# Starting two stationary operands at bytes 108 and 364 instead of 32 modulo 512

## The chip, the core and the metric

The kernel runs on one core of a Trainium2 chip. The metric is the device time of one execution in microseconds. In the profile PE is TensorE's matrix multiplication, PEld its loading of the stationary operand, DVE VectorE, ACT ScalarE, POOL GpSimd and SP SyncE. Each engine has its own stream of instructions and they wait for each other by semaphores; DMA queues move data between memory (HBM) and the on-chip memory (SBUF). SBUF has 128 partitions; a tile takes the same range of bytes in each of them, and "byte 32 modulo 512" below is where a tile's or a slice's range begins in every partition.

## What is computed

The reference is a two-layer decoder trunk on 256 tokens of width 2048, in float32. Each layer is a token mixer (layer 0 a gated DeltaNet, layer 1 HGRN2) followed by a SwiGLU block; each part is preceded by an RMSNorm and added to its input, and a last RMSNorm ends it:

```python
for layer in range(DEPTH):                       # DEPTH = 2
    h = h + mixer(rmsnorm(h, ...), ...)          # gated DeltaNet, then HGRN2
    h = h + swiglu(rmsnorm(h, ffn_norm[layer]), ffn_w_gate[layer], ffn_w_up[layer], ffn_w_down[layer])
return rmsnorm(h, final_norm)

def swiglu(h, w_gate, w_up, w_down):
    return (jax.nn.silu(h @ w_gate) * (h @ w_up)) @ w_down     # 2048 -> 5632 -> 2048
```

The change lies in the two SwiGLU blocks, in the product with `w_gate` and `w_up`.

## The kernel before

**High and low halves.** Every large product is computed from two halves of each operand: the high half is the float32 value rounded to the format that TensorE multiplies in one pass (`float32r`, a ScalarE copy), the low half what the rounding left out (a VectorE subtraction). A product takes three matmuls: high by high, high by low, low by high. Weights come by DMA in tiles of 128 x 1024 (`raw`, 512 KB) into four buffers, are split into `wh` and `wl` (four buffers each), and are used once. The tokens' halves stay on chip: `xt_h` and `xt_l`, four tiles each of 128 x (4 x 256), with the 2048 features along partitions and tiles and the 256 tokens along the free axis.

**Two ways of multiplying.** In `mm_rows` the tokens are stationary (128 x 128, loaded into TensorE) and 512 columns of weights stream past them. In `mm_cols` a 128 x 128 block of weights is stationary and the 256 tokens stream. `mm_cols` is used for part of the two mixers' input products (1024 triples of matmuls), `mm_rows` for nearly all else.

**Strassen's algorithm.** A SwiGLU block has 22 groups of 256 gate and 256 up columns, worked on in 11 pairs. Of each block, pairs 1, 4, 7 and 8 (`FF_PLAN`) are computed by a form of Strassen's algorithm with seven products in place of eight (`mixed_group`): the tokens are cut in two halves of 128, the features in two halves of 1024, the columns in gate and up. Three products (1, 2 and 4) take plain token halves from `xt_h` and `xt_l`. The other four (3, 5, 6 and 7) take sums of token blocks, which `mix_inputs` prepares once at the start of a block: VectorE forms the sums, ScalarE writes their high halves and VectorE their low halves into the tiles `mixh` and `mixl`, four sums of 1024 columns each. In every matmul of these groups the stationary operand is 128 columns of `mixh`, `mixl`, `xt_h` or `xt_l`, and the moving operand is 256 columns of `wh` or `wl`. The weights of products 4 to 7 are themselves sums, formed by VectorE in the weight tile before it is split. A group has four times four items; the `parts` of an item tell its products, so the items are: product 1; products 2 and 3 in turn; 5 and 7; 6 and 4 in turn. Each item has 6 or 12 matmuls, in triples that share a slice of tokens. `among` sets these items singly between the items (12 matmuls of 512 columns) of the plain pairs or of the down product.

**Order.** The program first records all operations. A planner (`plan`) then places them by modelled costs and due times into one order, which is issued engine by engine; weight tiles are prepared ahead of the matmuls, up to the number of buffers. The cost of an operation depends on its shape and not on where its tiles lie.

**Where tiles lie.** Pools are allocated in order, a tile after the other. A phase's pool (`ffn0`, `ffn1`) places its tiles in order of first use, with those whose size is no multiple of 512 bytes last (`open`). Constants are sized so that `xt_h` and `xt_l` begin at byte 32 modulo 512, and the phases' large tiles do too, `mixh` and `mixl` included (16,384 bytes each, first in their phase). The `wh` and `wl` buffers are longer by `PAD` = 64 words, and `make` shifts the slice that is used: for `mm_rows` and the mixed groups it begins at 32 modulo 512; for `mm_cols` at 108 (`wh`) and 364 (`wl`):

```python
PAD = 64
IN_COLS = {"wh": 108, "wl": 364}
...
at = 32 + n * v.pad * 4 % 512
want = IN_COLS[v.tag] if v.cols else 32 + n % 2 * 512
v.skip = (want - at) // 4
```

**Tail.** After the last down product `finish` and `finish_last` apply the last norm. They reuse the two tiles' places: `last` (the norm's weights, loaded by GpSimd's queue) in the place of `mixl`, and the output rows `y` in that of `mixh`.

The recorder calls one helper for all operations, so the profile has one line (L496) for nearly all instructions and the groups are told apart by the names of their tiles: `aux<-wh,mixh` is a matmul into `aux` with `wh` moving and `mixh` stationary.

Of the kernel before, what the change touches and what calls it, by code (L numbers as in the profile page):

```python
# [8 lines left out]
F32 = mybir.dt.float32  # L9
F32R = mybir.dt.float32r  # L10
# [7 lines left out]
P = 128  # L18
T = 256
D = 2048  # L20
# [61 lines left out]
PAD = 64  # L82
# [440 lines left out]
class Trunk:  # L523
# [308 lines left out]
    def mix_inputs(self):  # L832

        nc = self.nc

        def tt(out, a, b, op):
            nc.vector.tensor_tensor(out=out, in0=a, in1=b, op=op)

        self.mixed = [[], [], [], []]
        both = [self.tile(self.pool, [P, 4096], f"mix{x}", F32R) for x in "hl"]  # L840
        row = self.rstd_row.unsqueeze(1).broadcast_to([P, 4, T])
        for q in range(2):
            uv = []
            for cg in (q, 2 + q):
                t = self.tile(self.pool, [P, 4, T], "turned", bufs=2, ordered=True)
                tt(t, self.xt_h[cg].bitcast(F32), self.xt_l[cg].bitcast(F32), ALU.add)
                tt(t, t, row, ALU.mult)
                uv += [t[:, :, 0:P], t[:, :, P:T]]
            a11, a21, a12, a22 = uv
            sums = []  # L850
            for _ in range(2):
                t = self.tile(self.pool, [P, 2, 512], "h1", bufs=2, ordered=True)
                sums += [t[:, i, :].rearrange("p (k t) -> p k t", k=4) for i in range(2)]
            s1, s2, s3, s4 = sums
            tt(s1, a21, a22, ALU.subtract)
            tt(s2, a11, s1, ALU.subtract)
            tt(s3, a21, a11, ALU.subtract)
            tt(s4, a12, s2, ALU.subtract)
            for n in range(4):
                h, low = (  # L860
                    m[:, (2 * n + q) * 512 : (2 * n + q + 1) * 512].rearrange("p (k t) -> p k t", k=4)
                    for m in both
                )
                nc.scalar.activation(h, sums[n], AF.Copy)
                tt(low, sums[n], h.bitcast(F32), ALU.subtract)
                self.mixed[n].append((h, low))
# [994 lines left out]
    def finish(self, cg):  # L1861
        nc = self.nc
        if cg == 0:
            self.last = self.tile(self.pool, [P, 4096], "mixl", F32R, ordered=True).bitcast(F32)[:, 0:D]
            nc.gpsimd.dma_start(self.last, self.a["final_norm"].broadcast_to([P, D]))
            self.y = self.tile(self.pool, [P, 4096], "mixh", F32R, ordered=True).bitcast(F32).rearrange("p (t c) -> p t c", t=2)
            self.part = self.tile(self.pool, [P, 2], "part")
        self.sumsq(cg)
        c = slice(cg * 512, (cg + 1) * 512)
        nc.vector.tensor_tensor(  # L1870
            out=self.y[:, :, c], in0=self.x[cg], in1=self.last[:, c].unsqueeze(1).broadcast_to([P, 2, 512]),
            op=ALU.mult,
        )
        if cg == 2:
            nc.vector.tensor_reduce(
                out=self.part, in_=self.ssp[:, :, 0:3], axis=mybir.AxisListType.X, op=ALU.add
            )
            nc.vector.tensor_scalar(
                out=self.part, in0=self.part, scalar1=1.0 / D, scalar2=EPS, op0=ALU.mult, op1=ALU.add
            )  # L1880
# [130 lines left out]
```

## Time and profile before

| | |
|---|---|
| median of 3 runs | 2747.35 us (2745.71 to 2747.43) |
| the profiled execution | 2747.26 us |
| its span | 2745.6 us |
| TensorE busy, in matmuls | 2727.6 us, 16,822 instructions |
| weight loads | 2363.9 us, 16,822 instructions |
| VectorE busy | 2169.4 us |
| ScalarE busy | 1548.5 us |
| HBM traffic | 605.92 MB by DMA packets, mean 221 GB/s |
| mean granted TensorE clock | 0.998 |

The span runs from the first to the last instruction of the profiled execution; its own time is longer by what lies around the span. A row of a group reads: line, engine, operation, output<-inputs, array size, shape, count | busy us, mean ns of one | idle us of the engine just before, and what ended it. A matmul's duration reaches from its start to the end of its pipeline, so those of neighbours overlap, and the time that a matmul costs in a stream is the distance to the next one's start. A row of the view in order of time begins with the start in us and the duration in us.

### The profile page before, as it was taken

The page shows a single profiled execution, that of the slowest core. Times are in us where ns is not written, and L with a number is a line of the kernel's source. Part 1 is how long each engine was busy: PE and PEld are TensorE (multiplying, and loading weights), DVE is VectorE, ACT ScalarE, POOL GpSimd, SP SyncE. Part 2 cuts the span into 40 slices and gives each one's busy share as a digit, 9 for nine tenths or more (in the row PEclk, how much of TensorE's full clock was granted, in tenths as well). Part 3 has the DMA queues.
Part 4 walks back from the last instruction along what each step waited for, and adds up shares of the span by engine and source line. Part 5 has one row for each costly group of instructions (what it writes and reads, how often), then busy time and mean ns, then how long its engine had stood idle before and what let it go on. Part 6 is the DMA issues. An engine that isn't in the chain of part 4 may idle for free.

```text
span 2745.6 us, 44285 instructions
## 1 busy us (share of the span) xinstructions
PE 2727.6 (99%) x16822; PEld 2363.9 (86%) x16822; DVE 2169.4 (79%) x3309; ACT 1548.5 (56%) x2192; POOL 308.4 (11%) x466
## 2 busy tenths in 40 slices
PE   9999999999999999999999999999999999999998
PEld 9888888888888888888888989988888888888887
DVE  6778888877769898889857688778678898888665
ACT  6646666566555555555545556556455555555443
POOL 1213222232110000000000100000100000000000
PEclk9999999999999999999999999999999999999999
DMA  7686578686676667766676655555676667676764
GB/s 258 201 280 225 182 219 278 215 273 223 221 249 226 218 210 242 238 216 216 224 234 220 225 167 182 170 167 179 226 264 208 216 222 237 222 228 218 250 210 167
DMA packets 170375, 605.92 MB, mean 221 GB/s; under 512 B 21674, under 2 KB 22842, under 8 KB 170032
## 3 DMA queue, kind: packets, MB, share of 16 engines
q1 hardware_dynamic: 138912, 503.15, 55.9%
q0 software_dynamic: 30960, 99.08, 11.4%
q8 instruction: 132, 2.16, 0.3%
q10 hardware_dynamic: 288, 0.85, 0.1%
q14 instruction: 83, 0.68, 0.1%
HBM read 563.10 MB, written 39.89 MB: 220 GB/s over the span
## 4 chain that ended last, share of the span: by engine, by line
PE 98%; ACT 0%; DVE 0%; issue 0%; DMA 0%; SPq 0%; POOLq 0%; POOL 0%; ACTq 0%
PE main L496 81%; PE aux L496 18%; DMA first<-in_x 0%; ACT dec L496 0%; DVE wl L496 0%; ACT wh L496 0%; DVE utmp L496 0%; SPq L496 0%; DVE pre L496 0%; ACT xt_h L496 0%; DVE u L496 0%; ACT mixh L496 0%; POOLq L2007 0%; ACT junk L496 0%; DVE p L496 0%
## 5 line engine op out<-in xcount | busy, mean ns | idle before, releaser
L496 ACT ACTIVATE wh<-raw 128x1024 fp32r<-128x1024 f32 x817 | 864.4, 1059 | 937.9 <-PE main L496 803.2
L496 DVE TENSOR_TENSOR wl<-raw,wh 128x1024 fp32r<-128x1024 f32 x817 | 1003.1, 1229 | 426.4 <-ACT wh L496 416.8
L496 PE MATMUL main<-wh,xt_h 128*128 128x512 f32 x1664 | 651.8, 392 | 0.8 <-ACT wh L496 0.8
L496 PE MATMUL main<-wl,xt_h 128*128 128x512 f32 x1664 | 651.0, 391 | 1.3 <-DVE wl L496 1.3
L496 PE MATMUL main<-wh,xt_l 128*128 128x512 f32 x1664 | 650.6, 391 | 0.0
L496 PEld LDWEIGHTS main<-wh,xt_l 128*128 128x128 f32 x1664 | 312.6, 188 | 65.2
L496 PEld LDWEIGHTS main<-wh,xt_h 128*128 128x128 f32 x1664 | 312.9, 188 | 62.8 <-ACT wh L496 1.2
L496 PEld LDWEIGHTS main<-wl,xt_h 128*128 128x128 f32 x1664 | 312.9, 188 | 61.4 <-DVE wl L496 1.6
L496 ACT ACTIVATE wh<-sraw 128x1024 fp32r<-128x1024 f32 (+1 forms) x256 | 243.4, 951 | 141.6 <-PE main L496 98.1
L496 DVE TENSOR_TENSOR wl<-sraw,wh 128x1024 fp32r<-128x1024 f32 (+1 forms) x256 | 278.4, 1088 | 28.2 <-ACT wh L496 26.8
L496 PE MATMUL main<-xt_h,wh 128*128 128x256 f32 (+1 forms) x1040 | 289.5, 278 | 0.7 <-ACT wh L496 0.7
L496 PE MATMUL main<-xt_h,wl 128*128 128x256 f32 (+1 forms) x1040 | 288.9, 278 | 0.9 <-DVE wl L496 0.9
L496 PE MATMUL main<-xt_l,wh 128*128 128x256 f32 (+1 forms) x1040 | 288.7, 278 | 0.3 <-DVE xt_l L496 0.3
L496 PE MATMUL main<-wh,hth 128*128 128x512 f32 x680 | 266.7, 392 | 1.0 <-ACT hth L496 1.0
L496 PE MATMUL main<-wl,hth 128*128 128x512 f32 x680 | 266.2, 391 | 0.0
L496 PE MATMUL main<-wh,htl 128*128 128x512 f32 x680 | 265.5, 390 | 0.1
L496 PEld LDWEIGHTS main<-xt_h,wh 128*128 128x128 f32 (+1 forms) x1040 | 194.8, 187 | 1.3 <-ACT wh L496 0.9
L496 PEld LDWEIGHTS main<-xt_h,wl 128*128 128x128 f32 (+1 forms) x1040 | 194.7, 187 | 1.2 <-DVE wl L496 1.1
L496 PEld LDWEIGHTS main<-xt_l,wh 128*128 128x128 f32 (+1 forms) x1040 | 194.7, 187 | 1.0 <-DVE xt_l L496 0.5
L496 PEld LDWEIGHTS main<-wh,htl 128*128 128x128 f32 x680 | 127.7, 188 | 29.1 <-DVE htl L496 1.7
L496 PE MATMUL main<-wh,ot_l 128*128 128x512 f32 x384 | 151.4, 394 | 0.0
L496 PE MATMUL main<-wh,ot_h 128*128 128x512 f32 x384 | 150.6, 392 | 0.0
(238 smaller groups left out, 4094.0 us busy)
## 6 DMA issues: line engine op xcount, KB each, us to landing
raw<-in_ffn_gu SPq DMA_DIRECT2D x224, 512.0 KB, 4.6
raw<-in_ffn_d SPq DMA_DIRECT2D x176, 512.0 KB, 4.6
sraw<-in_ffn_gu SPq DMA_DIRECT2D x128, 512.0 KB, 5.1
raw<-in_hgrn_in SPq DMA_DIRECT2D x128, 512.0 KB, 3.9
raw<-in_gdn_kq SPq DMA_DIRECT2D x64, 512.0 KB, 5.7
raw<-in_gdn_v SPq DMA_DIRECT2D x64, 512.0 KB, 4.8
raw<-in_gdn_z SPq DMA_DIRECT2D x64, 512.0 KB, 4.8
raw<-in_gdn_out SPq DMA_DIRECT2D x64, 512.0 KB, 5.0
```

The lines of the kernel that those rows point to most:

```text
L496: getattr(getattr(tc.nc, op.eng), op.method)(*args, **kw)
```

## The change

The tiles `mixh` and `mixl` become 64 words longer, and the sums are written to and read from words 19 to 4114 of them. With the place that the allocator then gives the tiles (last in their phase, 16,640 bytes each), the high halves begin at byte 108 and the low halves at byte 364 modulo 512, and so does every 128-column slice, since the slices are multiples of 512 bytes apart. The other tiles of the phase move down by 32,768 bytes and keep their place modulo 512. `finish` takes the longer tiles and uses them from their first word: `last` lies at 288 and `y` at 32 modulo 512. No instruction is added or removed, and the planner's order is the same.

```diff
@@ mix_inputs
-        both = [self.tile(self.pool, [P, 4096], f"mix{x}", F32R) for x in "hl"]
+        both = [self.tile(self.pool, [P, 4096 + PAD], f"mix{x}", F32R)[:, 19 : 19 + 4096] for x in "hl"]
@@ finish
-            self.last = self.tile(self.pool, [P, 4096], "mixl", F32R, ordered=True).bitcast(F32)[:, 0:D]
+            self.last = self.tile(self.pool, [P, 4096 + PAD], "mixl", F32R, ordered=True).bitcast(F32)[:, 0:D]
             nc.gpsimd.dma_start(self.last, self.a["final_norm"].broadcast_to([P, D]))
-            self.y = self.tile(self.pool, [P, 4096], "mixh", F32R, ordered=True).bitcast(F32).rearrange("p (t c) -> p t c", t=2)
+            self.y = self.tile(self.pool, [P, 4096 + PAD], "mixh", F32R, ordered=True).bitcast(F32)[:, 0:4096].rearrange("p (t c) -> p t c", t=2)
```

## The prediction

> **What bounds the kernel now.** I read the page first (share of the span, then the chain), then the groups by form of TensorE, then the two FFN stretches by engine, and last single matmuls in order of time.
>
> ```profile
> span 2745.6 us, 44285 instructions
> PE 2727.6 (99%) x16822; PEld 2363.9 (86%) x16822; DVE 2169.4 (79%) x3309; ACT 1548.5 (56%) x2192; POOL 308.4 (11%) x466
> PE 98%; ACT 0%; DVE 0%; issue 0%; DMA 0%; SPq 0%; POOLq 0%; POOL 0%; ACTq 0%
> ```
>
> The chain that ends last is 98% TensorE. What shortens a matmul's turn on TensorE shortens the kernel, as long as the engines that feed it keep up. The operands of the change belong to the groups below (stationary operand last in the name), with their weight loads; beside them stand the only other groups whose moving operand also has 256 columns.
>
> ```profile
> L496 PE MATMUL main<-xt_h,wh 128*128 128x256 f32 x1024 | 284.3, 278 | 0.7 <-ACT wh L496 0.7
> L496 PE MATMUL aux<-wh,mixh 128*128 128x256 f32 x512 | 144.4, 282 | 0.0
> L496 PE MATMUL aux<-wl,mixh 128*128 128x256 f32 x512 | 144.9, 283 | 0.0
> L496 PE MATMUL aux<-wh,mixl 128*128 128x256 f32 x512 | 145.0, 283 | 0.0
> L496 PE MATMUL aux<-wh,xt_h 128*128 128x256 f32 x384 | 108.1, 282 | 0.0
> L496 PEld LDWEIGHTS main<-xt_h,wh 128*128 128x128 f32 x1024 | 192.3, 188 | 1.3 <-ACT wh L496 0.9
> L496 PEld LDWEIGHTS aux<-wh,mixh 128*128 128x128 f32 x512 | 97.9, 191 | 4.4
> L496 PEld LDWEIGHTS aux<-wh,xt_h 128*128 128x128 f32 x384 | 73.3, 191 | 4.4
> ```
>
> So 3 x 512 = 1536 matmuls have a sum of tokens as the stationary operand, and TensorE sat idle 0.0 us before them. By the program's layout, every operand of the `aux` rows starts at byte 32 modulo 512, stationary and moving alike. In the `main<-xt_h,wh` row the stationary operand is a weight tile at 108 (`wh`) or 364 (`wl`), and the moving one, the tokens, is at 32. There the load takes 188 ns against 191, the matmul 278 against 282. These durations overlap; the cost is the distance between starts. Matmuls in order of time, first a run of 12 on sums between 512-column matmuls, then one that alternates sums and plain tokens:
>
> ```profile
> 1005.64 0.39 PE L496 MATMUL main<-wh,htl 128*128 128x512 f32 x1
> 1005.87 0.28 PE L496 MATMUL aux<-wh,mixh 128*128 128x256 f32 x1
> 1005.98 0.28 PE L496 MATMUL aux<-wl,mixh 128*128 128x256 f32 x1
> 1006.10 0.28 PE L496 MATMUL aux<-wh,mixl 128*128 128x256 f32 x1
> ...
> 1007.18 0.28 PE L496 MATMUL aux<-wh,mixl 128*128 128x256 f32 x1
> 1007.30 0.40 PE L496 MATMUL main<-wh,hth 128*128 128x512 f32 x1
> ...
> 1010.28 0.28 PE L496 MATMUL aux<-wh,mixl 128*128 128x256 f32 x1
> 1010.40 0.28 PE L496 MATMUL aux<-wh,xt_h 128*128 128x256 f32 x1
> ...
> 1011.36 0.28 PE L496 MATMUL aux<-wh,xt_l 128*128 128x256 f32 x1
> 1011.48 0.40 PE L496 MATMUL main<-wh,hth 128*128 128x512 f32 x1
> ```
>
> From 1006.10 to 1007.30 are 10 matmuls in 1.20 us: 120 ns each; from 1010.40 to 1011.48 are nine, half sums and half plain tokens, in 1.08 us: 120 ns again. The start of a run is cheaper: 1005.87 to 1006.10 is 0.23 us for two matmuls instead of 0.24, so a run of 12 takes 1.43 us. Between the roundings I take 7 ns. Now the run with weights stationary at 108 and 364, which also enters from 512 columns:
>
> ```profile
> 471.38 0.39 PE L496 MATMUL main<-wh,ot_l 128*128 128x512 f32 x1
> 471.61 0.28 PE L496 MATMUL main<-xt_h,wh 128*128 128x256 f32 x1
> ...
> 471.96 0.28 PE L496 MATMUL main<-xt_h,wh 128*128 128x256 f32 x1
> ...
> 482.73 0.28 PE L496 MATMUL main<-xt_h,wl 128*128 128x256 f32 x1
> ```
>
> The first three take 0.35 us, 117 ns each. From the fourth to the last of these 99 are 95 distances in 10.77 us: 113.4 ns. Same shape, same engine, 6.6 ns less a matmul once settled; 3 x 3.9 = 12 ns more in all on entering.
>
> **The change part by part.** (a) *The sums' address.* Both tiles grow by 64 words (256 bytes) and the sums begin 19 words in. As their size is then no multiple of 512, the allocator puts them behind the phase's other large tiles: `mixh` at 32 + 76 = 108, `mixl` 16,640 bytes further, at 288 + 76 = 364. That is the phase of `wh` and `wl` in the 113.4 ns run: stationary 76 (or 332) bytes past the moving operand, modulo 512. I take the settled price of that run for the 1536 matmuls: 1536 x (120 - 113.4) = 10.1 us less.
>
> Three corrections, by the order of the work. In each of 16 mixed groups (2 FFN blocks x 4 pairs x 2) there are four times four items: product 1 (6 matmuls on tokens); products 2 and 3 (tokens, sums, tokens, sums, three each); 5 and 7 (12 on sums); 6 and 4 (sums, tokens, sums, tokens). That is 64 items of each kind, nearly all between 512-column items.
> - Items that begin with sums (64 of 5/7, 64 of 6/4) lose the cheap start of today, 7 ns each: 0.9 us back.
> - Each entry into sums costs the 12 ns of three slow pairs: 2 entries in a 2/3 item, 1 in a 5/7 item, 2 in a 6/4 item, 320 in all: 3.8 us back. No row shows an entry from plain tokens at 32; the entry from a 512-column run (tokens' stationary at 32 too) is the nearest. Ends: nothing, or 6.6 ns on every matmul of the 256 triples in mixed items (768 x 6.6 = 5.1 us), where they would never settle.
> - A switch from sums back to tokens (1 inside a 2/3 item, 2 in a 6/4 item: 192) resembles the entry from 512 columns into a run at 32, which is 7 ns cheap: 1.3 us more gained. Ends: 0, or all 1152 token matmuls at 113.4 (7.6 us).
>
> Sum: 10.1 - 0.9 - 3.8 + 1.3 = **6.7 us** less.
>
> (b) *The feeding engines.* The saved time must not be lost to a late weight tile.
>
> ```profile
> 873.00:1084.00 211.00, 210.74 (x1191) 184.75 (x1190) 186.69 (x249) 116.61 (x132) 11.19 (x19) 1.00 0.68 222
> 2072.00:2290.00 218.00, 217.73 (x1232) 191.08 (x1231) 191.64 (x255) 120.27 (x136) 11.18 (x19) 1.00 0.69 222
> ACT wh L496 <- PE main L496: 901.4, 619, 6.3
> ```
>
> The windows (PE, PEld, DVE, ACT, POOL busy, clock, DMA share, GB/s) are two mixed stretches: PE 210.7 of 211 us at clock 1.00, DVE 186.7, DMA 0.68. ScalarE's splits wait for TensorE to free buffers, 901.4 us in all: supply runs ahead. With PE some 0.8% shorter there, DVE goes from 88 to 89%: still cover. If it weren't, the whole gain would go, not more; VectorE would be late next.
>
> (c) *Moves.* All other FFN tiles slide down 32,768 bytes, 64 x 512: their phases stay. Plan, engine order, waits and DMAs are untouched; no instruction is added. Cost 0; the cover is that every overlapped tile of the former phase was already read by the matmuls that the tokens of the new phase come from.
>
> (d) *Writes and other reads at the new phase.* 16 ScalarE and 16 VectorE writes of the sums, and in the tail `last` at 288 instead of 32:
>
> ```profile
> L496 ACT ACTIVATE mixh<-h x16: 611/616/623, 844.3 to 2084.1; 128x512 fp32r<-128x512 f32 x16
> L496 DVE TENSOR_TENSOR mixh<-x,mixl x3: 1218/1219/1225, 2687.9 to 2721.5; 128x1024 f32<-128x1024 f32 x3
> L496 ACT ACTIVATE wh<-raw x63: 1042/1062/1068, 22.7 to 198.0; 128x1024 fp32r<-128x1024 f32 x63
> L496 ACT ACTIVATE wh<-raw x48: 1042/1060/1063, 1002.1 to 1194.8; 128x1024 fp32r<-128x1024 f32 x48
> ```
>
> The last two are weight splits in a stretch with many tiles at 108 and in one with all at 32: 1062 and 1060 ns. So 0. Bounds: 2 ns each way on 37 instructions, under 0.1 us, and matmuls cover all but the tail.
>
> The profiled execution took 2747.26 us (span 2745.6), beside the shown median of 2747.35: 2747.3 - 6.7 = **2740.6 us**.
>
> **The rivals.**
> 1. *Short triples never settle.* Only long stretches gain: 12 x 6.6 - 12 - 7 = 60 ns in each 5/7 item, 64 x 60 = 3.8 us: 2743.5. For it: the slow entry at 471.61. Against: that entry was over after three.
> 2. *The address is not the cause.* In the fast run the moving tokens rest in memory and weights are stationary; here it is the reverse. Then nothing moves: 2747.3. Against: 32/32 is slow in runs on resting tokens and on sums alike.
>    The Trainium skill ("SBUF — State Buffer", Who interferes with whom) gives TensorE two independent read ports, for matmul and weight load: by it the starts of the operands shouldn't matter, and the time would be 2747.3. The traces' 120 against 113.4 ns stands against it but, with operands swapped, not conclusively.
> 3. *Slower: the crooked start.* 108 and 364 are 12 past a multiple of 16, so a 512-byte read touches 33 pieces of 16 bytes instead of 32. If each such load and its matmul stretch by 1/32, 120 / 32 = 3.75 ns x 1536 = 5.8 us: 2753.1. It decides as soon as a pair on sums takes over 120 ns. Against: the `wh` loads at that very start take 188 ns, fewer than 191.
>    The Trainium skill (same page, Specifications) says that each crossing to a new 16-byte line costs something; the 188 disagrees as far as it goes.
> 4. *More: the phase carries over.* Plain tokens between sums also fall to 113.4: up to 10.1 + 7.6 = 17.7 us, 2729.6; with half of the tokens, and the entry costs still paid, 10.1 - 0.9 - 3.8 + 3.8 = 9.2: 2738.1.
>
> **How the numbers follow.** A change under 0.2% (5.5 us) can hardly be told from none here. Forecast 0.59, rival 1 0.13, rival 2 0.10, rival 3 0.11, rival 4 0.07. The forecast's own range is 2736.8 to 2743 (entry costs from 0 to 1.6 times mine); 0.09 of its 0.59 lies past 2741.9 and so short of 0.2%. Faster: 0.50 + 0.07 = 0.57; same: 0.09 + 0.13 + 0.10 = 0.32; slower: 0.11. The range runs from just under the forecast's own to just over no change; it leaves out rival 3 and the far half of rival 4: 2736.5 to 2747.8.
>
> **What would show it.** Right: `mixh` and `mixl` loads near 188 ns and their matmuls near 278; the 12-run down from 1.43 to about 1.37 us; 512-column rows as before, DVE's busy time unchanged, the tail too. The entry costs show in the first three pairs of every triple. Wrong: pairs on sums at 120 or more, a changed distance in the 512-column runs, or PE waiting for `wl`.

## The result

The changed kernel takes 2739.68 us (median of nine runs, 2738.99 to 2741.25), the kernel before 2746.08 us (nine runs, 2745.71 to 2747.84). The ratio is 0.9977, with a 95% interval from 0.9968 to 0.9986: 6.4 us less, where 6.7 us less were forecast and 2740.6 us as the time. The profiled execution took 2739.51 us, beside 2747.26 us before.

The page of the changed kernel, with the span, the busy times and the chain that ended last:

```profile
span 2737.7 us, 44285 instructions
PE 2719.8 (99%) x16822; PEld 2355.8 (86%) x16822; DVE 2168.5 (79%) x3309; ACT 1549.2 (57%) x2192; POOL 307.6 (11%) x466
PE 96%; DVE 2%; ACT 1%; issue 1%; POOLq 0%; POOL 0%; DVEq 0%; ACTq 0%
```

TensorE's matmuls lost 7.8 us of busy time and its weight loads 8.1 us; VectorE and ScalarE are as busy as they were. The groups by form of the changed kernel:

```profile
L496 PE MATMUL main<-xt_h,wh 128*128 128x256 f32 x1024 | 284.1, 277 | 0.7 <-ACT wh L496 0.7
L496 PE MATMUL aux<-wh,mixh 128*128 128x256 f32 x512 | 142.6, 279 | 0.0
L496 PE MATMUL aux<-wh,mixl 128*128 128x256 f32 x512 | 142.3, 278 | 0.0
L496 PE MATMUL aux<-wh,xt_h 128*128 128x256 f32 x384 | 108.0, 281 | 0.0
L496 PEld LDWEIGHTS aux<-wh,mixl 128*128 128x128 f32 x512 | 96.3, 188 | 0.0
L496 PEld LDWEIGHTS aux<-wh,xt_l 128*128 128x128 f32 x384 | 73.2, 191 | 0.0
```

The sums' loads are at 188 to 189 ns (191 before), their matmuls at 278 and 279 (282 and 283): close to the 188 and 277 ns of the fast group in the first row. The loads of plain tokens stay at 191. In order of time, a run of 12 on sums and one that alternates, both at the same places of the work as the two shown of before:

```profile
1003.41 0.28 PE L496 MATMUL aux<-wh,mixh 128*128 128x256 f32 x1
...
1003.77 0.28 PE L496 MATMUL aux<-wh,mixh 128*128 128x256 f32 x1
...
1004.79 0.40 PE L496 MATMUL main<-wh,hth 128*128 128x512 f32 x1
1005.02 0.40 PE L496 MATMUL main<-wl,hth 128*128 128x512 f32 x1
...
1007.53 0.28 PE L496 MATMUL aux<-wh,mixh 128*128 128x256 f32 x1
...
1008.95 0.40 PE L496 MATMUL main<-wh,hth 128*128 128x512 f32 x1
```

The first three matmuls of the 12 take 0.36 us and the other nine 1.02 us, 113 ns each; the run takes 1.38 us instead of 1.43. The alternating run (sums, tokens, sums, tokens) takes 1.42 us. Read from all starts in the two traces, the 1536 distances behind matmuls on sums add up to 177.4 us instead of 183.5, and those on plain tokens in the mixed items lose 0.5 us more: 6.6 us in all. The starts also show where the kernel became shorter. From its first mixed item to its last, each of the two FFN blocks takes 502.0 us instead of 505.2, 6.3 us less in both together (their 512-column matmuls, with the waits among them, take 0.3 us more). The 694.2 us between these two stretches and the 168.0 us behind them didn't change. The profiled spans differ by 7.9 us because 1.5 us more lie ahead of the first mixed item (at 871.5 us instead of 873.1), where the change touches no matmul; this start varies between 871.4 and 873.0 us in later traces that change no matmul ahead of it either.

The feeding engines kept up. The first two rows are TensorE's longest waits, the third one of the mixed stretches (PE, PEld, DVE, ACT, POOL busy, clock, DMA share, GB/s):

```profile
PE main L496 <- DVE wl L496: 2.2, 2, 1.3
PE main L496 <- ACT wh L496: 1.5, 2, 0.8
871.40:1081.50 210.10, 209.75 (x1194) 183.81 (x1193) 187.04 (x250) 116.88 (x133) 11.19 (x19) 1.00 0.69 224
```

The same two waits had 2.2 and 1.5 us before; DVE is at 187.0 of 210.1 us, 89%. That the chain now shows VectorE with 2% is a near tie in its reading and no new wait of TensorE.

### The profile page after: what moved, and what is told of

Its sections match the earlier page's. It is cut to its first block, busy times and chain, and to the rows that moved or that the text cites. A ratio compares the mean times of both kernels' runs of the same rounds, so it can differ in the third digit from the quotient of the medians.

```text
span 2737.7 us, 44285 instructions
## 1 busy us (share of the span) xinstructions
PE 2719.8 (99%) x16822; PEld 2355.8 (86%) x16822; DVE 2168.5 (79%) x3309; ACT 1549.2 (57%) x2192; POOL 307.6 (11%) x466
## 3 DMA queue, kind: packets, MB, share of 16 engines
q0 software_dynamic: 30960, 99.08, 11.3%
## 4 chain that ended last, share of the span: by engine, by line
PE 96%; DVE 2%; ACT 1%; issue 1%; POOLq 0%; POOL 0%; DVEq 0%; ACTq 0%
PE main L496 80%; PE aux L496 17%; DVE wl L496 1%; DVE turned L496 1%; ACT wh L496 0%; ACT dec L496 0%; DVE htl L496 0%; DVE sraw L496 0%; ACT xt_h L496 0%; DVE h L496 0%; DVE utmp L496 0%; DVE pre L496 0%; DVE u L496 0%; ACT mixh L496 0%; POOLq L2007 0%
```

## The experiments

Three theories were open after the result. D: the distance between the start of the stationary and of the moving operand sets the price of a pair (0 is slow, 76 is fast). P: the place of the stationary operand alone does. And the rival that the address isn't the cause at all. Later runs add W, S and E, on what it is about 108 that helps: its place within 16 bytes (W), its place within 64 bytes (S), or only 108 itself modulo 256 (E). Single profiled runs below stand beside a run of the kernel before on the same chip, 2746.1 us in the first two groups and 2748.2 us in the third; a single run can be off by a microsecond or two, so their verdicts rest on distances between starts.

### One half alone

```diff
-[:, 19 : 19 + 4096] for x in "hl"]
+[:, s : s + 4096] for x, s in (("h", 19), ("l", 64))]     # high halves at 108, low halves at 32
+[:, s : s + 4096] for x, s in (("h", 0), ("l", 19))]      # the other run: 32 and 364
```

> Only the high halves of the sums start at 108; the low halves are back at 32 (modulo 512). Theory D (the distance between stationary and moving start sets the price of a pair, 0 is slow, 76 is fast): 1024 of 1536 matmuls are fast once settled. If each pair simply has its own price, a settled triple costs 113.4 + 113.4 + 120 ns, a 12-run about 1.39 us, and the kernel about two thirds of the change's gain: 2742. If the slow entry of three pairs starts anew whenever a low half breaks the row, nothing settles: triples near 117 + 118 + 120, 12-run about 1.42, time about 2745. Theory P (the place of the stationary operand alone counts) expects the first of these.

> Only the low halves start at 364, the high halves are at 32. Own price for each pair: a settled triple 120 + 120 + 113.4, a 12-run about 1.41 us, time about 2744. If entries start anew: no gain, 2746. If the price of a pair is set by the load that runs beside it (that of the next stationary operand), the fast distance is the one in front of the matmul on the low half and not the one behind it.

The times are 2743.32 and 2743.13 us. A 12-run with the high halves alone, then one with the low halves alone (first matmul, and the 512-column matmul behind the run):

```profile
1003.96 0.28 PE L496 MATMUL aux<-wh,mixh 128*128 128x256 f32 x1
...
1005.37 0.40 PE L496 MATMUL main<-wh,hth 128*128 128x512 f32 x1
```

```profile
1004.45 0.28 PE L496 MATMUL aux<-wh,mixh 128*128 128x256 f32 x1
...
1005.86 0.39 PE L496 MATMUL main<-wh,hth 128*128 128x512 f32 x1
```

Both take 1.41 us. Two thirds of the fast starts bring no more than one third: all 1536 distances together fall by 1.9 us with the high halves and by 2.8 us with the low ones, against 6.15 with both. A pair has no price of its own. With the high halves alone the distances of a 12-run go 118, 118, 128, 122, 117, 118, 113, 114, 120, 113, 113, 119: a break in the row costs more than 120 at first, and the two settled triples at the end have the 113, 113, 120 of the expectation, with the slow one in front of the next high half. The low halves alone leave a steady 118, 118, 117; their 12-run has the 1.41 us that a price of each pair would give, but that would be 120, 120, 113.

### Four bytes more

```diff
-[:, 19 : 19 + 4096] for x in "hl"]
+[:, s : s + 4096] for x, s in (("h", 20), ("l", 20))]     # 112 and 368
```

> The sums start at 112 and 368: 80 bytes past the moving operand instead of 76, now on a multiple of 16. Theory D with a coarse distance (any start well apart will do): as the change, settled pairs at 113.4 ns, 2739.7. Theory C (the crooked start itself, 12 past a multiple of 16, is what helps): settled pairs back at 120, 2746. If the distance has to be exact, anything between, or worse than 120.

```profile
1003.92 0.28 PE L496 MATMUL aux<-wh,mixh 128*128 128x256 f32 x1
...
1005.34 0.40 PE L496 MATMUL main<-wh,hth 128*128 128x512 f32 x1
```

The time is 2743.59 us and the 12-run takes 1.42 us, behind its first two pairs at 117 to 120 ns each: all distances on sums fall by 1.0 us instead of 6.15, so four bytes lose most of the gain. It will not do that the starts are merely well apart.

### The weights moved instead of the sums

```diff
-            want = IN_COLS[v.tag] if v.cols else 32 + n % 2 * 512
+            want = (None, IN_COLS, IN_MIXED)[v.cols][v.tag] if v.cols else 32 + n % 2 * 512
+IN_MIXED = {"wh": 212, "wl": 468}     # for the weights of the mixed items; sums and tokens at 32
...
+            where = 1 if item.cols else 2 if item.ring else 0     # 2: the mixed items
```

> The sums are back at 32 and the kernel is the one before, but the weight tiles of the mixed items start at 212 (high) and 468 (low) modulo 512, so that every stationary operand of these items, sums and plain tokens alike, is 76 bytes past the moving one modulo 256. Theory D: all 2688 pairs fall to 113.4 ns, and only the entry from 512 columns costs 12 ns and loses 7 (some 220 runs): 2688 x 6.6 - 220 x 19 = 13.6 us less than before, 2732.5. Theory P: the stationary operands are at 32, so all pairs stay at 120 and the time at 2746.

```profile
1005.36 0.28 PE L497 MATMUL aux<-wh,mixh 128*128 128x256 f32 x1
...
1006.79 0.40 PE L497 MATMUL main<-wh,hth 128*128 128x512 f32 x1
```

The time is 2744.61 us and the 12-run 1.43 us, no shorter than before the change: after three pairs the distances alternate between 117 and 123 ns, whether the stationary operand is a sum or plain tokens. D in its simple form fell: the same distance at other places gives nothing. P held here. The two mixed stretches are 2.5 us shorter than before all the same, and that came from the 512-column matmuls behind the mixed items: the first four take 233, 231, 227, 227 instead of 233, 236, 228, 233.

### Other starts, two in each run

Each FFN block has its own tiles, so one run shows two starts.

```diff
-[:, 19 : 19 + 4096] for x in "hl"]
+[:, s : s + 4096] for x in "hl" for s in [(3, 23)[j]]]     # words, by block j; also (35, 18) and (0, 16)
```

> The change with another start in each FFN block: 44 and 300 in the first (12 bytes past the moving operand modulo 256), 124 and 380 in the second (92 bytes). What the change's 108 shares with them: all are 12 past a multiple of 16; 44 is 64 less, so it is also the same modulo 64, 124 is not. Theory W (the place within 16 bytes decides): both blocks settle at 113.4 ns, as in the change, 2739.7. Theory S (the place within 64 bytes decides): the first block settles at 113.4, the second does not, about 2743. Theory E (108 modulo 256 exactly): neither, 2744 to 2747.

> Starts at 172 and 428 in the first FFN block (140 bytes past the moving operand, 64 more than in the change, so the same within 64 bytes), at 104 and 360 in the second (72 bytes, 4 less than in the change, 8 past a multiple of 16). Theory W: the first block settles at 113.4 ns, the second doesn't. Theory S: the same. Theory E: neither. If 4 bytes less does no harm (80 did), the second block settles too and the price depends on a limit between 76 and 80.

> Starts on multiples of 16: 32 and 288 in the first FFN block (0 and 256 bytes past the moving operand), 96 and 352 in the second (64 bytes). Theories W, S and E: both blocks stay near 120 ns, 2746. If 256 bytes between high and low halves count by themselves, the first block moves. If any wide distance had helped, the second would be fast.

A 12-run of each block, for 12 and 92, then 140 and 72, then 0 and 64 bytes past 32:

```profile
974.61 0.28 PE L496 MATMUL aux<-wh,mixh 128*128 128x256 f32 x1
...
976.02 0.40 PE L496 MATMUL main<-wh,xt_h 128*128 128x512 f32 x1
...
2172.47 0.28 PE L496 MATMUL aux<-wh,mixh 128*128 128x256 f32 x1
...
2173.89 0.40 PE L496 MATMUL main<-wh,xt_h 128*128 128x512 f32 x1
```

```profile
975.91 0.28 PE L496 MATMUL aux<-wh,mixh 128*128 128x256 f32 x1
...
977.35 0.40 PE L496 MATMUL main<-wh,xt_h 128*128 128x512 f32 x1
...
2175.24 0.28 PE L496 MATMUL aux<-wh,mixh 128*128 128x256 f32 x1
...
2176.66 0.39 PE L496 MATMUL main<-wh,xt_h 128*128 128x512 f32 x1
```

```profile
974.84 0.28 PE L496 MATMUL aux<-wh,mixh 128*128 128x256 f32 x1
...
976.28 0.40 PE L496 MATMUL main<-wh,xt_h 128*128 128x512 f32 x1
...
2173.90 0.28 PE L496 MATMUL aux<-wh,mixh 128*128 128x256 f32 x1
...
2175.32 0.40 PE L496 MATMUL main<-wh,xt_h 128*128 128x512 f32 x1
```

In bytes past the moving start: 12 gives 1.41 us, 64 1.42, 72 1.42, 92 1.42, 140 1.44 and 0 1.44 (1.433 us at the trace's full resolution for both), against 1.38 at 76. None of the six settles at 113.4 ns. W and S fell, E stood: of the starts tried only 76 is fast. The first block of the last run differs from the kernel before in the low halves, at 288 instead of 32, and has its 1.43 us: 256 bytes make no difference. Since all tiles lie there where the change put them, the allocator's move of the tiles isn't the cause of the gain either. The times are 2744.02, 2746.83 and 2744.75 us. The run with 140 and 72 bytes gains 1.5 us on the sums and 0.8 us on the tokens and gives it back: its 512-column matmuls cost 2.3 us more than before, in the first ones behind a mixed item, and its mixed stretches take 505.1 us each, as long as before.

### The tokens at 108 and 364, too

```diff
-        self.xt_h = [t([P, 4, T], f"xt_h{i}", F32R) for i in range(4)]
-        self.xt_l = [t([P, 4, T], f"xt_l{i}", F32R) for i in range(4)]
+        parts = lambda x: [x[:, 19 + i * 4 * T : 19 + (i + 1) * 4 * T].rearrange("p (k t) -> p k t", k=4) for i in range(4)]
+        self.xt_h = parts(t([P, 16 * T + PAD], "xt_h", F32R))
+        self.xt_l = parts(t([P, 16 * T + PAD], "xt_l", F32R))
```

A second edit, not printed, lets an operation wait for the part of the longer tile that it reads and not for the whole tile; the order of TensorE's matmuls is the same.

> The change, and the tokens' own tiles start at 108 (high) and 364 (low) too; same order of instructions. In the mixed items every stationary operand then has the start that is fast: all 2688 pairs settle at 113.4 and no entry from plain tokens is left; 384 us of the kernel's pairs by W, S and E alike, about 9 us less than the change in these items. The 512-column matmuls on tokens (4992) get a stationary operand at 108 instead of 32: if the 13 ns that they take over 512 columns have the same cause, they fall from 227 to about 220, up to 33 us less; if not, they stay at 227. The matmuls with stationary weights at 108 now have moving tokens at 108 and 364: if the stationary place alone counts they stay at 113.4, if the two starts have to differ they go to 120, 20 us more.

(The 384 us in it is a slip: 2688 pairs at 120 ns are 323 us.) The time is 2785.53 us, 39 us more than before. The groups of this kernel:

```profile
L497 PE MATMUL aux<-wh,mixh 128*128 128x256 f32 x512 | 142.0, 277 | 0.0
L497 PE MATMUL aux<-wh,xt_h 128*128 128x256 f32 x384 | 106.7, 278 | 0.0
L497 PE MATMUL main<-xt_h,wh 128*128 128x256 f32 x1024 | 290.2, 283 | 0.2 <-ACT wh L497 0.2
L497 PE MATMUL main<-wh,xt_h 128*128 128x512 f32 x1664 | 659.3, 396 | 0.4 <-ACT wh L497 0.4
L497 PE MATMUL main<-wh,hth 128*128 128x512 f32 x680 | 266.5, 392 | 1.2 <-ACT hth L497 1.2
```

This one run decides three questions. Plain tokens in the mixed items are now fast (278 ns, distances of 113 once settled; sums and tokens of the mixed items together 11.3 us under before), so it is the start and not what the tile holds. The matmuls with stationary weights at 108 and moving tokens at 108 went from 113.4 to 120 ns, 283 ns in duration, 19 us in all: a stationary start at 108 is not enough, it must stand off from the moving one, so P fell as well. And the 512-column matmuls on tokens take 234 ns instead of 227 (396 against 391 in duration), 27.6 us in all, while those on `hth`, still at 32, are unchanged: for 512 columns this distance is a loss.

### Both operands 128 bytes further

```diff
-[:, 19 : 19 + 4096] for x in "hl"]
+[:, 51 : 51 + 4096] for x in "hl"]                        # sums at 236 and 492
+IN_MIXED = {"wh": 160, "wl": 416}                         # weights of the mixed items, used as in the run that moved them
```

> The change with both operands of the mixed items 128 bytes further: weights move from 160 and 416, sums stand at 236 and 492, so the distance is 76 modulo 256 as in the change and the moving start is again a multiple of 32. If the distance decides (and the moving start at 212 spoilt the run with moved weights because it is no multiple of 16): 12-runs on sums settle at 113.4 ns, about 1.39 us. If the two places themselves count (32 against 108): 12-runs at 1.41 to 1.43 us. Plain tokens stay at 32, 128 bytes before the moving start: no row shows their price; the whole time is left open, 2738 to 2748.

```profile
1003.55 0.28 PE L497 MATMUL aux<-wh,mixh 128*128 128x256 f32 x1
1003.67 0.28 PE L497 MATMUL aux<-wl,mixh 128*128 128x256 f32 x1
...
1004.92 0.39 PE L497 MATMUL main<-wh,hth 128*128 128x512 f32 x1
1005.14 0.39 PE L497 MATMUL main<-wl,hth 128*128 128x512 f32 x1
1005.37 0.39 PE L497 MATMUL main<-wh,htl 128*128 128x512 f32 x1
1005.60 0.39 PE L497 MATMUL main<-wh,hth 128*128 128x512 f32 x1
```

The 12-run settles after one slow pair, takes 1.37 us, and the 512-column matmuls behind it run at 227 ns at once, where they took 233, 236, 228, 233 and 231 before. So 108 itself, as E has it, is not needed, and D stands again with a condition: the distance of 76 is fast at 32 and 108 and at 160 and 236, and not at 212 and 288 (which is 32 modulo 256). The first two moving starts are multiples of 32; 212 isn't one of 16. That this is the condition was not tested by itself. Plain tokens, 128 bytes before the moving start, take 117 to 123 ns. The time is 2738.54 us, against 2748.19 for before on the same chip.

### A better start for 512 columns?

```diff
+ROWS = {"in_gdn_v": 4, "in_gdn_z": 8, "in_gdn_out": 16, "in_ffn_gu0": 2, "in_ffn_d0_0": 1, ...}   # words past 32
+            v.skip = ROWS[v.cols] if v.cols in ROWS else (want - at) // 4
...
```

> The change, and the moving weights of the 512-column matmuls start elsewhere, another place for each group of weights: 4, 8, 12, 16, 32, 48, 64, 80, 96, 128, 160, 180 and 224 bytes past 32, against stationary operands at 32. Settled matmuls take 227 ns at distance 0; the tokens' tiles at 108 showed 234 at the other sign. If the 13 ns over the 512 columns are the same thing as the 6.6 ns of the 256-column pairs, some of these places take about 220 ns; if 32 against 32 is already the best for 512 columns, all take 227 to 240 and the kernel is slower, 2740 to 2790.

The time is 2787.10 us. Distances between settled 512-column matmuls, from the starts in the trace, mean for the high and low halves of each group:

```
bytes past 32     4   8  12  16  32  48  64  80  96 128 160 180 224     0
ns a matmul     239 233 229 232 233 232 229 231 233 233 234 238 233   227
```

Nothing is under the 227 of distance 0 (those at 12 and 64 come nearest). So 32 against 32 is the best of these starts for 512 columns, though not for 256.

### A version ahead of both, and the change again

```diff
+            where = 1 if item.cols else 2 if item.ring and not item.part else 0     # product 1 alone keeps 32
```

The rest as in the run with both operands 128 bytes further.

> As the run with both operands 128 bytes further (12-runs on sums at 1.365 us and no slow 512-column matmuls behind them), but the items of product 1, on plain tokens alone, keep moving weights at 32 and with that 713 ns for six and the usual exit. By the runs of each item in those traces: 48 x 48 ns for the items on sums alone, 56 x 19 ns for those that begin with sums, 40 x 11 ns lost on those that begin with tokens, together some 2.9 us less than the change: 2736.8 where the change takes 2739.7. If the rest of the kernel drifts with such shifts, anything from 2735 to 2740.

> The change once more, beside the run above on the same chip: 6.4 us less than before, ratio 0.9977, as in its first comparison.

On the same chip before took 2746.85 us (16 runs), the change 2740.88 (11 runs; ratio 0.9979, 0.9970 to 0.9988), this version 2738.73 (six runs; 0.9969, 0.9956 to 0.9981). Every one of its six runs (2737.65 to 2739.22) is under every one of the change (2739.75 to 2743.44). The change's gain is confirmed, and its mixed stretches take 502.0 us each as in its first trace. By the medians the other place brings 2.2 us more; the mixed stretches, 501.2 us each, show 1.7 us of it. They don't come from the settled price, which is the same: all distances on sums add up to 177.6 us, beside the change's 177.4. They come from the pairs on plain tokens (1.3 us) and the 512-column matmuls behind the mixed items (0.7 us). The expectation's terms of 48, 19 and 11 ns were too large: from the two traces, they are some 33 (6 within a 12-run, 27 behind it), 7 and 7 ns.

## Why the prediction was right

- *The address decides, with the price of the weight-stationary run.* Right: 113.4 ns forecast, 113.3 measured in settled runs on sums. The rival that the address isn't the cause fell with the tokens at 108, and with the starts 0 and 256 bytes off, where all tiles lie as in the change and the 1.43 us are back. The crooked start costs nothing: at 108, 44 and 124, all 12 past a multiple of 16, a pair in a 12-run takes 114.5, 117 and 118 ns on average, less than the 119.4 of before. The rival that plain tokens become fast as well fell too: they lose 0.5 us in all, of the 7.6 us that it would have meant.
- *Entry costs of 12 ns.* Near for the entry from 512 columns: 117.5, 118.4 and 118.3 at the start of a 12-run, 14 ns over three settled pairs. Entering from plain tokens, for which there was no row, costs 7 ns and not 12: the first of the three slow pairs is the last one on tokens, at 118 instead of 120, two on sums are at 117 to 118, and the third pair on sums is settled. The rival that only long stretches gain fell with that.
- *Cheap start lost, cheap switch back.* The cheap start was lost as forecast. The cheap switch back did not come: the first pair on tokens behind settled sums takes 119.2 ns and the next 120, under 1 ns saved where 7 were forecast, so the term of 1.3 us is nearly nothing. That the sum still holds is luck: the 192 switches back were counted 1.2 us too cheap and the 192 entries from tokens 0.9 us too dear. The items show it. Lone items took, in ns, 1433 before; after, 1374 for products 5 and 7 (59 saved, 60 forecast), 1407 for 2 and 3 (26 saved, 23 forecast by the same terms) and 1420 for 6 and 4 (13 saved, 23 forecast). 64 x (59 + 26 + 13) ns = 6.3 us; at 16 places two items on sums follow one another without 512 columns between them, which saves 21 ns more each time, 0.3 us. That makes 6.6 us, beside the forecast's 6.7.
- *Nothing else moves.* Right: the 512-column matmuls cost 0.2 us less in the trace (distances under 0.3 us, without waits), VectorE 2168.5 us against 2169.4; the writes of the high halves take 616 ns as before, and TensorE's last matmul ends 10.0 us ahead of the span's end in both.
- *The feeding engines keep up.* Right, by TensorE's unchanged waits.
- *A gain past what a measurement can tell from none.* Just so: 0.23% less, with the interval at 0.14 to 0.32%.

The forecast leaned on one distance, taken over whole from another run. The experiments show how lucky such a transfer has to be: 4 bytes beside it most of the gain is gone, and with the moving operand at 212 all of it is. Why 76 bytes are fast was not forecast and is not shown.

## What to carry to other kernels

Where TensorE is the bound and every load of a stationary operand serves one matmul, measure the distance between starts and not the durations, and compare groups of the same shape whose operands start at different bytes. A start that is fast for one width can be slow for another: 76 bytes gave 113 instead of 120 ns at 256 columns and 234 instead of 227 ns at 512. Count the runs as well as the matmuls: each change of pattern costs two or three slow pairs, and here that took a third of the 10.1 us that the settled price alone would have saved (6.6 us were left).

## What the runs showed of the hardware

- In these traces (granted clock 0.997 to 0.999) TensorE's price of a load and matmul depends on where both operands start. With 256 columns, average distances in a 12-run go from 114 ns (76 bytes apart, with the moving start at 32 or 160) over 117 (12 bytes) and 118 (64, 72, 80, 92) to 119.4 (0, 140, 256). 4 bytes count (72 and 80 against 76), while 256 bytes make no difference to 0. The Trainium skill ("SBUF — State Buffer", Who interferes with whom) has two independent read ports on TensorE, one for loads and one for the moving operand, and TensorE waiting for no one. That gives the starts no reason to matter, but the traces show that they do: settled pairs take 120 ns with both operands at 32 or both at 108, and 113.3 to 113.4 ns with the stationary one at 108 and the moving one at 32.
- A stretch of 256-column matmuls leaves a mark on the 512-column ones behind it: 233, 236, 228, 233 and 231 ns instead of 227 in the kernel before, 26 ns in all, with the stationary start at 32 or at 108; some 45 ns after 12-runs on sums 12, 92 or 140 bytes off; nothing after 12-runs on sums at 236 with weights at 160.
- The mechanism behind 76 stays open. No counter in these traces shows the reads of on-chip memory, and the alternation of 117 and 123 ns with weights at 212 averages to the 120 ns of before.
